# A two-layer decoder kernel: another order of the attention steps, other top-k rounds, paired value products and more warming matmuls

## The chip, the cores and the metric

The kernel runs on one core of one Trainium2 chip. The metric is the device time of a launch in microseconds (us). The core has a matrix engine (TensorE; PE in the profile, and PEld for its weight loads), a vector engine (VectorE, DVE), an activation engine (ScalarE, ACT), a general engine (GpSimd, POOL) and queues that start DMA transfers, of which SyncE's (SP) carries nearly all.

## The reference

The input is 512 tokens of 1024 channels in float32. Layer 0 is attention, layer 1 a spatial gating unit; behind each stands a gated feed-forward network (FFN) with a short causal convolution, and a final norm ends it. The change lies in layer 0's attention, which mixes two parts and projects their concatenation:

```python
h = rmsnorm(x, g)
proj = h @ w_in
aq, ak, av, ar, alr, bq, bk, bv, iq, ik, iw = split_cols(proj, IN_WIDTHS)
log_a = jax.nn.log_sigmoid(alr @ w_a2 + b_a) / GLA_GATE_TAU
oa = gla_chunked(aq, ak, av, log_a)                 # gated linear attention, 4 heads
oa = rmsnorm(oa, head_g) * jax.nn.silu(ar)
bq, bk, iq, ik = (rope_partial(a, pos) for a in (bq, bk, iq, ik))
# sparse attention, 8 heads that share one key and one value of width 64
score = sum_h iw[h] * relu(iq[h] @ ik.T)            # 4 indexer heads, causal
idx = top_k(score, 128)                             # the keys that a query may see
ob = softmax(bq @ bk[idx].T / 8) @ bv[idx]
x = x + concat([oa, ob]) @ w_o
```

## The kernel before

Activations lie with channels on the 128 partitions and the 512 tokens along the row. Weights come in chunks of 128 x 1024 on SP's queue, two chunks ahead of their use; ScalarE casts each to a high part (L148) and VectorE, or GpSimd for the names in `ON_POOL`, subtracts to get the low part (L149). A product of float32 numbers is then three matmuls (L160 to L162). Buffers: two raw chunks, three pairs of parts, four PSUM banks for long accumulations (`pacc`) and four for short ones (`paux`).

A few matmuls on zeros come first (`WARM`, L111). Four chunks of w_in give the indexer's queries and keys, the key, the value and some narrow columns (`p_first`). Each further chunk of w_in is taken by `chan` (one bank, 24 matmuls of 512 columns) or, four chunks at a time, by `tokens` (four banks at once, 96 matmuls).

The steps of the attention are named, with the token block or tile as a digit: QK (queries and keys of the linear attention), LG and DC (its logits and decays, `logits` and `decays`), AV (its values), ST (states), GL (its output), AR and GT (gates), BQ (queries of the sparse attention, with RoPE in `halves` and four copies on SP's queue in `queries`), SC (indexer scores), TC (top-k), W (softmax weights, `weigh`) and A (value products, `gather`). A round of top-k finds the eight largest scores of each query and strikes them out (`topk`, L349 and L350). It takes sixteen rounds for each of the token blocks 1, 2 and 3; each TC does four rounds for all three.

`ORDER` lists the steps in the order of preference. A scheduler at build time turns this list into one fixed stream of instructions per engine: it takes an instruction when a model of times says that it can run, and the list decides between those that can. So the list shifts priorities; it is not the order itself, and an engine executes its stream strictly in order. In `gather`, each pair of tiles of weights is transposed, copied out of PSUM (L541 or L543) and multiplied by the values (L545); the two products of a pair write the lower and the upper 64 partitions of one bank. `SWAPPED` names the tiles for which ScalarE and VectorE change places in `weigh` (L524 to L527) and in those copies. After the steps, `out_half` multiplies the first half of w_o with the linear attention's output and then the second half with the sparse attention's.

Of the kernel before, what the change touches and what calls it, by code (L numbers as in the profile page):

```python
# [26 lines left out]
LOOKAHEAD = 2  # L27
WARM = 9
ORDER = ("QK0 SC1 QK1 SC2 SC3 LG QK2 DC0 QK3 DC1 BQ0 BQ1 BQ2 TC2 BQ3 TC3 AV ST1 "
         "ST0 GL0 GL3 TC1 GL2 GL1 AR GT1 GT0 GT2 GT3 W0 TC0 W3 A0 W1 W2 A3 A1 A2")  # L30
MIX_LAG = 4
SPREAD = 3
# what GpSimd does in place of VectorE; where ScalarE and VectorE change places
ON_POOL = {
# [4 lines left out]
}  # L39
SWAPPED = {  # L40
# [3 lines left out]
}  # L44
# [3 lines left out]
def trunk(ctx: ExitStack, tc: tile.TileContext, I, out):  # L48
# [10 lines left out]
    paux = ctx.enter_context(tc.tile_pool(name="paux", bufs=4, space=PSUM))  # L59

    def slot(name, dt=F32):
        return spool.tile([P, T], dt, tag="s", name=name)
# [12 lines left out]

    # ---- inputs that stay
    pg = cst.tile([P, 40], F32, name="pg")
    nc.scalar.dma_start(pg, I["gains"])
    pv = cst.tile([P, I["pv"].shape[1]], F32, name="pv")
    nc.gpsimd.dma_start(pv, I["pv"])  # L80
    x = [xpool.tile([P, T], F32, tag="x", name=f"x{d}") for d in range(KD)]
    con = cst.tile([P, 3, P], F32, name="con")
    nc.gpsimd.dma_start(con, I["con"])
    ident, cmask, gmask = con[:, 0, :], con[:, 1, :], con[:, 2, :]
# [15 lines left out]
    def gate_b(i):  # L100
        o = 264 + 88 + i
        return pv[:, o:o + 1]

    one = cst.tile([P, 1], F32, name="one")
    V.memset(one, 1.0)
# [9 lines left out]

    # ---- weights: loaded in chunks of [128, 1024], each split into two float32r parts
    order = []
    for name, n in (("w_in", 20), ("w_o", 8), ("w_up0", 44), ("w_dn0", 24), ("w_uv", 16),
                    ("w_out", 8), ("w_up1", 44), ("w_dn1", 24)):
        for c in range(n):  # L120
            cols = 768 if name.startswith("w_dn") and c % 3 == 2 else 1024
            if name.startswith("w_dn"):
                src = I["w_dn"][int(name[4]), c // 3][:, 1024 * (c % 3):1024 * (c % 3) + cols]
            elif name.startswith("w_up"):
                src = I["w_up"][int(name[4]), c]
            else:
                src = I[name][c]
            order.append((f"{name}_{c}", src, cols))
    ready = {}
    state = {"made": 0, "used": 0}  # L130

    def make_chunk():
# [6 lines left out]
        if i < 4:  # L139
            for k2 in range(2):  # L140
                w = slice(k2 * T, (k2 + 1) * T)
                nc.sync.dma_start(x[2 * i + k2], I["xT"][2 * i + k2])
                nc.sync.dma_start(raw[:, w], src[:, w])
                S.copy(h[:, w], raw[:, w])
                V.tensor_sub(l[:, w], raw[:, w], h[:, w])
        else:
            nc.sync.dma_start(raw[:, :cols], src)
            S.copy(h[:, :cols], raw[:, :cols])  # L148
            eng(name).tensor_sub(l[:, :cols], raw[:, :cols], h[:, :cols])  # L149
# [13 lines left out]

    # ---- the normed stream: x * gain in two parts, and 1/rms of each token
    class Normed:
# [25 lines left out]
    def residual(d, ps, step):  # L191
        """x[d] += ps, then the next norm's step on it; the last one is what all wait for."""
        with tc.high_priority() if d == KD - 1 else nullcontext():
# [29 lines left out]
    def chan(n, name):  # L223
        """A chunk's 128 channels by all tokens, before 1/rms."""
        wh, wl = chunk()
# [10 lines left out]
    def tokens(n, name):  # L236
        """Four chunks' 512 channels, by blocks of tokens, before 1/rms."""
        ps = [acc(f"{name}{b}") for b in range(NB)]
# [13 lines left out]

    # ---- layer 0: attention
    n0 = normed()
# [12 lines left out]
    lo, hi = slice(0, 64), slice(64, P)  # L267
    CS = [slot("rope_c"), slot("rope_s")]
    for i in range(2):
        nc.gpsimd.dma_start(CS[i], I["rope"][i])  # L270

    def halves(ps, cs, name):
        """A tile after its rotation, in two parts."""
        t1 = slot("rope1")
# [12 lines left out]
    def queries(ps, cs, dst, name):  # L287
        """dst[e] = head e's high part over its low part."""
        h, l = halves(ps, cs, name)
# [4 lines left out]
    def dots(ps, q, ks):  # L294
        """All four products of the parts."""
        PE.matmul(ps, q, ks[0], start=True, stop=False)
# [28 lines left out]

    mask = [cmask]

    def scores(b):
        n = P * (b + 1)
        t = slice(b * P, (b + 1) * P)  # L330
        sc = slot(f"score{b}")
        mask.append(sc[:, :n])
        for h in range(4):
# [20 lines left out]

    # gated linear attention
    def queries_keys(i):
# [144 lines left out]

    # sparse attention
    def heads(i):
# [25 lines left out]
    def gather(b):  # L529
# [3 lines left out]
        for st in range(b + 1):  # L533
            pT = []
            for e in range(2):
# [4 lines left out]
                if bool(e) != (f"pT{b}{st}{e}" in SWAPPED):  # L540
                    S.copy(pT[e], pt)  # L541
                else:
                    V.tensor_copy(pT[e], pt)  # L543
            for e in range(2):
                PE.matmul(po[64 * e:64 * e + 64, :], tok[:, st, 0:64], pT[e], start=st == 0, stop=st == b)  # L545
        split(lazy("bh", [P, 4, T], F32R)[:, :, t], lazy("bl", [P, 4, T], F32R)[:, :, t],
              po.rearrange("p (j c) -> p j c", c=P))

    picked = [0] * NB
    # the steps of layer 0 in the order that the scheduler prefers  # L550
    steps = {"QK": queries_keys, "SC": scores, "LG": logits, "DC": decays, "BQ": heads, "AV": values,
             "ST": states, "GL": gla, "AR": gates, "GT": gate, "W": weigh, "A": gather,
             "TC": lambda i: topk((1, 2, 3), 4)}
    for name in ORDER.split():
        step = steps[name.rstrip("0123")]
        i = name[len(name.rstrip("0123")):]
        step(int(i)) if i else step()

# [17 lines left out]

    # ---- gated conv FFN
    def ffn(l, n, nxt, gi):
# [52 lines left out]
    def close(n, ps, t):  # L631
        """The last residual, final norm and store of 256 tokens."""
        with tc.high_priority():
# [35 lines left out]

    # ---- layer 1: spatial gating  # L670
    v = [big(f"v{b}", [P, 2, T]) for b in range(NB)]
# [66 lines left out]
def _layout(inp):  # L738
# [6 lines left out]
    def by_k(w):  # L745
        """[K, n] -> [128, K / 128, n]"""
        return w.reshape(w.shape[0] // P, P, w.shape[1]).transpose(1, 0, 2)
# [35 lines left out]
    A["w_s"] = f["sgu_w_s"][0].transpose(2, 0, 1)  # L783
    # constants of the shapes
    i = np.arange(P)
# [33 lines left out]
```

## Time and profile before

| | us |
|---|---|
| median of three runs | 1124.99 |
| lowest and highest run | 1124.42, 1126.47 |
| profiled execution, span | 1124.9 |
| TensorE busy | 1099.9 |
| VectorE busy | 717.1 |
| ScalarE busy | 451.2 |
| GpSimd busy | 100.8 |

The profiled execution is told by its span alone, from the first to the last instruction; the page has no other time of it. The first 257.5 us are layer 0's attention, the rest the two FFNs and layer 1.

How to read the rows further down: a row of a timeline has the start in the span, the busy time, the engine, the line, the operation and its tiles and how many instructions are merged (x2); in brackets stands how long the engine was idle before, and what ended that. A row of stretches has, for each engine, the busy time and the number of instructions, then TensorE's granted clock as a share of 2.4 GHz, the DMA engines' busy share and GB/s. Matmuls overlap in the records, so their pitch is read from their starts or their count.

### The profile page before, as it was taken

Reading aid. Unit: us, or ns where it says so; the run is one execution under the profiler, and the core shown is the slowest. Engines: PE = TensorE matmul, PEld = TensorE weight load, DVE = VectorE, ACT = ScalarE, POOL = GpSimd, SP = SyncE. Lnnn points to the kernel's source line nnn. Section 1 sums busy time; section 2 is a strip of 40 time slices with the busy share of each in tenths; the row PEclk is TensorE's granted clock in tenths of the full one; section 3 lists DMA queues with packets and bytes.
Section 4 is the critical chain, followed back from the end, with each engine's and each line's share of the span. In section 5 each row is a group of like instructions: output and inputs, shape, how many; then the busy total and the mean of one; then the engine's idle time right before and its main releaser. Section 6 shows DMA issues by size and latency. Waiting matters only on the chain.

```text
span 1124.9 us, 13026 instructions
## 1 busy us (share of the span) xinstructions
PE 1099.9 (98%) x5043; PEld 893.1 (79%) x5043; DVE 717.1 (64%) x1112; ACT 451.2 (40%) x649; POOL 100.8 (9%) x71
## 2 busy tenths in 40 slices
PE   8997999999999999999999999999999999999997
PEld 6875767487888888888888888888888888888886
DVE  5799789667777777753333385766777777753222
ACT  6452249144444444432222333435444444433221
POOL 1454240040000000000000000120000000000001
PEclk9998999999999999999999999999999999999999
DMA  6615120122222332223333523222233322233322
GB/s 225 187 38 150 57 68 9 38 94 94 94 94 95 103 102 95 94 85 103 99 94 108 169 75 113 76 94 94 94 96 104 100 94 94 94 103 87 101 85 75
DMA packets 34925, 108.86 MB, mean 97 GB/s; under 512 B 4160, under 2 KB 6480, under 8 KB 34864
## 3 DMA queue, kind: packets, MB, share of 16 engines
q1 hardware_dynamic: 33536, 104.87, 29.4%
q10 hardware_dynamic: 1040, 2.27, 0.7%
q8 instruction: 39, 0.64, 0.2%
q0 software_dynamic: 288, 0.90, 0.2%
q14 instruction: 22, 0.18, 0.0%
HBM read 101.73 MB, written 2.10 MB: 92 GB/s over the span
## 4 chain that ended last, share of the span: by engine, by line
PE 92%; DVE 5%; ACT 1%; issue 1%; DMA 0%; POOL 0%; POOLq 0%; SPq 0%; DVEq 0%; ACTq 0%
PE p_up L161 14%; PE p_up L162 14%; PE p_up L160 14%; PE p_dn L162 7%; PE p_dn L161 7%; PE p_dn L160 7%; PE po L545 1%; PE p_v L246 1%; PE p_so L160 1%; PE p_so L161 1%; PE p_u L160 1%; PE p_v L248 1%; PE p_u L161 1%; PE p_so L162 1%; PE p_u L162 1%; PE p_v L247 1%
## 5 line engine op out<-in xcount | busy, mean ns | idle before, releaser
L160 PE MATMUL p_up<-xh,h_w_up 128*128 128x512 f32 x704 | 274.3, 390 | 0.7 <-ACT xh L173 0.7
L161 PE MATMUL p_up<-xl,h_w_up 128*128 128x512 f32 x704 | 274.0, 389 | 0.6 <-DVE xl L174 0.6
L162 PE MATMUL p_up<-xh,l_w_up 128*128 128x512 f32 x704 | 273.9, 389 | 0.0
L160 PEld LDWEIGHTS p_up<-xh,h_w_up 128*128 128x128 f32 x704 | 132.1, 188 | 28.3 <-ACT xh L173 1.1
L161 PEld LDWEIGHTS p_up<-xl,h_w_up 128*128 128x128 f32 x704 | 132.1, 188 | 28.3 <-DVE xl L174 0.9
L162 PEld LDWEIGHTS p_up<-xh,l_w_up 128*128 128x128 f32 x704 | 132.1, 188 | 27.4
L161 PE MATMUL p_dn<-g,h_w_dn 128*128 128x512 f32 (+1 forms) x374 | 140.9, 377 | 0.0
L160 PE MATMUL p_dn<-g,h_w_dn 128*128 128x512 f32 (+1 forms) x374 | 140.9, 377 | 0.0
L162 PE MATMUL p_dn<-g,l_w_dn 128*128 128x512 f32 (+1 forms) x374 | 140.9, 377 | 0.0
L149 DVE TENSOR_TENSOR l_w_dn<-raw_w_dn,h_w_dn 128x1024 fp32r<-128x1024 f32 (+1 forms) x48 | 54.5, 1136 | 107.7 <-ACT h_w_dn L148 107.6
L148 ACT CAST h_w_up<-raw_w_up 128x1024 fp32r<-128x1024 f32 x88 | 92.7, 1054 | 62.5 <-PE p_up L161 47.7
L587 DVE TENSOR_TENSOR a<-p_up,R 128x512 f32<-128x512 f32 x88 | 60.5, 688 | 84.5 <-PE p_up L162 79.3
L149 DVE TENSOR_TENSOR l_w_up<-raw_w_up,h_w_up 128x1024 fp32r<-128x1024 f32 x87 | 106.5, 1224 | 9.4 <-ACT h_w_up L148 7.0
L148 ACT CAST h_w_dn<-raw_w_dn 128x1024 fp32r<-128x1024 f32 (+1 forms) x48 | 47.2, 983 | 147.8 <-PE p_dn L161 143.4
L160 PEld LDWEIGHTS p_dn<-g,h_w_dn 128*128 128x128 f32 x374 | 70.4, 188 | 13.0
L161 PEld LDWEIGHTS p_dn<-g,h_w_dn 128*128 128x128 f32 x374 | 70.4, 188 | 12.9
L162 PEld LDWEIGHTS p_dn<-g,l_w_dn 128*128 128x128 f32 x374 | 70.4, 188 | 12.8
L599 ACT CAST g<-c 128x512 fp32r<-128x512 f32 x44 | 27.3, 621 | 116.8 <-DVE c L596 116.8
L589 ACT ACTIVATE c<-a,pv 128x512 f32<-128x512 f32 x88 | 71.7, 815 | 2.9 <-DVE a L587 2.3
L592 DVE SCALAR_TENSOR_TENSOR c<-a,pv,c 128x510 f32<-128x510 f32 x88 | 65.9, 749 | 3.0
L590 DVE SCALAR_TENSOR_TENSOR c<-a,pv,c 128x511 f32<-128x511 f32 x88 | 65.6, 745 | 1.8 <-ACT c L589 1.8
L595 ACT ACTIVATE c<-c 128x512 f32<-128x512 f32 x44 | 27.8, 632 | 82.6 <-DVE c L592 82.6
(259 smaller groups left out, 1620.2 us busy)
## 6 DMA issues: line engine op xcount, KB each, us to landing
raw_w_up<-in_w_up SPq DMA_DIRECT2D x88, 512.0 KB, 3.3
raw_w_dn<-in_w_dn SPq DMA_DIRECT2D x32, 512.0 KB, 3.4
raw_w_in<-in_w_in SPq DMA_DIRECT2D x16, 512.0 KB, 3.6
raw_w_uv<-in_w_uv SPq DMA_DIRECT2D x16, 512.0 KB, 3.4
raw_w_dn<-in_w_dn SPq DMA_DIRECT2D x16, 384.0 KB, 3.1
raw_w_o<-in_w_o SPq DMA_DIRECT2D x8, 512.0 KB, 3.3
raw_w_out<-in_w_out SPq DMA_DIRECT2D x8, 512.0 KB, 3.4
x<-in_xT SPq DMA_DIRECT2D x8, 256.0 KB, 5.1
```

What stands on the lines that cost most here:

```text
L148: S.copy(h[:, :cols], raw[:, :cols])
L149: eng(name).tensor_sub(l[:, :cols], raw[:, :cols], h[:, :cols])
L160: PE.matmul(ps, wh, xh, start=start, stop=False)
L161: PE.matmul(ps, wh, xl, start=False, stop=False)
L162: PE.matmul(ps, wl, xh, start=False, stop=stop)
L246: PE.matmul(ps[b], n.h[k][:, t], wh[:, w], start=k == 0, stop=False)
L587: V.tensor_mul(a, ps, n.R)
L589: S.activation(cc, a, AF.Identity, bias=conv_b(l, m), scale=conv_w(l, m, 2))
L590: V.scalar_tensor_tensor(cc[:, 1:], a[:, :T - 1], conv_w(l, m, 1), cc[:, 1:], op0=ALU.mult, op1=ALU.add)
L592: V.scalar_tensor_tensor(cc[:, 2:], a[:, :T - 2], conv_w(l, m, 0), cc[:, 2:], op0=ALU.mult, op1=ALU.add)
L595: S.activation(c[0], c[0], AF.Silu)
L599: S.copy(gh, c[1])
```

## The change

It warms with 20 matmuls where there were 9. The order of steps is another one, and TC gives way to steps T that name their blocks (T12 does four rounds for blocks 1 and 2). The chunks of w_in are loaded by the order in which the new list uses them. Constants, RoPE tables and per-channel values are loaded on SP's queue behind the third chunk, no longer on GpSimd's. The first product of a pair in `gather` also waits for the second tile's copy. Two lists of who computes what have other members.

```diff
-WARM = 9
-ORDER = ("QK0 SC1 QK1 SC2 SC3 LG QK2 DC0 QK3 DC1 BQ0 BQ1 BQ2 TC2 BQ3 TC3 AV ST1 "
-         "ST0 GL0 GL3 TC1 GL2 GL1 AR GT1 GT0 GT2 GT3 W0 TC0 W3 A0 W1 W2 A3 A1 A2")
+WARM = 20
+ORDER = ("QK0 LG BQ2 SC2 SC1 T12 QK1 BQ3 QK3 QK2 DC1 DC0 SC3 BQ0 AV ST0 BQ1 ST1 GL0 GL1 "
+         "T123 GL2 T23 GL3 AR GT1 GT0 T1 T23 GT2 GT3 W0 T3 W3 T1 W1 W2 A1 A3 A2 A0")
...
 ON_POOL = {
-    "gate0", "gate2", "gate3", "ka0", "ka1", "qa1", "qa2", "rabq1", "rabq2",
-    "rabq3", "rakk", "rcs0", "rcs1", "rmiq1", "rsbq0", "rsbq2", "rsbq3", "rsiq0",
-    "ss2", "ss3", "w_in_10", "w_in_11", "w_in_12", "w_in_14", "w_in_15", "w_in_17", "w_in_18",
-    "w_in_4", "w_in_8", "w_o_0", "w_o_1", "w_o_5", "w_up0_1",
+    "gate0", "gate2", "gate3", "ka1", "qa2", "rabq1", "rabq3", "raiq1", "rcs1", "rmbq0",
+    "rmbq2", "rmbq3", "rmiq0", "rmiq1", "rmkk", "rsbq0", "rsbq1", "rsiq0", "ss3",
+    "w_in_12", "w_in_15", "w_in_18", "w_in_4", "w_in_6", "w_in_7", "w_in_9", "w_o_0",
+    "w_o_1", "w_o_3", "w_o_5", "w_o_6",
 }
 SWAPPED = {
-    "nm01", "nm02", "nm03", "nm10", "nm12", "nm13", "nm14", "nm16", "nm22",
-    "nm24", "nm25", "nm30", "nm32", "nm33", "nm34", "pT001", "pT101", "pT111",
-    "pT200", "pT201", "pT211", "pT221", "pT301", "pT311", "pT321", "pT331",
+    "nm03", "nm14", "nm33", "pT111",
 }
...
+    def together(i, other):
+
+        tc.add_manual_dep(i.ins, other.ins.name,
+                          mybir.DependencyInfo(mybir.DependencyClass.Sync, mybir.DependencyReason.DATA),
+                          reason="together")
...
+    at = {"QK1": [5], "QK2": [6], "QK3": [7], "BQ0": [8], "BQ1": [9], "BQ2": [10], "BQ3": [11],
+          "AV": [12, 13, 14, 15], "AR": [16, 17, 18, 19]}
+    order[5:20] = [order[i] for name in ORDER.split() for i in at.get(name, ())]
...
+            if i == 2:
+                for t, src in ((con, I["con"]), (CS[0], I["rope"][0]), (CS[1], I["rope"][1]), (pv, I["pv"])):
+                    nc.sync.dma_start(t, src)
...
             for e in range(2):
-                PE.matmul(po[64 * e:64 * e + 64, :], tok[:, st, 0:64], pT[e], start=st == 0, stop=st == b)
+                i = PE.matmul(po[64 * e:64 * e + 64, :], tok[:, st, 0:64], pT[e][0], start=st == 0,
+                              stop=st == b)
+                if e == 0:
+                    together(i, pT[1][1])
```

## Rows read from the trace of the kernel before

**Rows 1.** The page's totals: busy us, share of the span and instructions of each engine

```profile
PE 1099.9 (98%) x5043; PEld 893.1 (79%) x5043; DVE 717.1 (64%) x1112; ACT 451.2 (40%) x649; POOL 100.8 (9%) x71
```

**Rows 2.** Stretches, by stage: PE, PEld, DVE, ACT, POOL, PEclk, DMA share, GB/s

```profile
30.90:80.00 49.10, 49.02 (x215) 38.83 (x213) 40.44 (x60) 27.81 (x44) 23.56 (x15) 0.97 0.38 104
80.00:107.00 27.00, 18.78 (x59) 13.72 (x59) 27.00 (x65) 5.42 (x7) 15.89 (x10) 0.81 0.53 148
107.00:163.90 56.90, 56.27 (x342) 42.21 (x340) 47.20 (x140) 15.86 (x45) 16.74 (x11) 1.00 0.21 65
163.90:169.20 5.30, 2.43 (x19) 2.05 (x19) 4.60 (x8) 3.57 (x6) 3.05 (x2) 1.00 0.39 131
169.20:228.50 59.30, 59.23 (x279) 38.21 (x280) 44.70 (x150) 29.92 (x85) 2.40 (x1) 1.00 0.07 25
...
257.50:1124.90 867.40, 859.27 (x3911) 715.18 (x3909) 515.03 (x642) 336.41 (x415) 22.80 (x19) 1.00 0.31 97
```

**Rows 3.** Stretches right behind pauses of TensorE, and one of steady products

```profile
7.38:10.98 3.60, 3.60 (x10) 2.82 (x10) 2.17 (x4) 2.47 (x5) 0.00 (x0) 0.57 1.04 407
11.00:30.80 19.80, 19.80 (x88) 16.43 (x87) 14.23 (x23) 12.16 (x20) 2.40 (x1) 0.99 0.60 206
...
93.10:97.00 3.90, 3.69 (x8) 2.46 (x8) 3.90 (x11) 1.19 (x2) 1.78 (x2) 0.56 0.42 97
100.80:107.00 6.20, 6.17 (x15) 4.85 (x16) 6.20 (x20) 1.67 (x2) 3.99 (x4) 0.51 0.71 226
```

**Rows 4.** Timeline of TensorE at the start

```profile
1.23 3.71 PE L112 MATMUL ps_warm<-warm 128*128 128x512 bf16 x9 [1.23 <-DVE mhalf L114]
7.38 0.82 PE L160 MATMUL p_first<-xh,h_w_in 128*128 128x512 f32 x2 [2.44 <-ACT h_w_in L144]
```

**Rows 5.** Timeline of TensorE, 78 to 132 us: the rows with a pause ahead

```profile
80.99 0.50 PE L162 MATMUL p_bq<-xh,l_w_in 128*128 128x512 f32 x1 [0.92 <-POOL l_w_in L149]
...
93.18 0.78 PE L246 MATMUL p_av<-h_w_in,xh 128*128 128x512 f32 x1 [3.72 <-DVE rope L278]
...
98.91 0.50 PE L248 MATMUL p_av<-l_w_in,xh 128*128 128x512 f32 x1 [2.04 <-DVE l_w_in L149]
100.83 0.79 PE L246 MATMUL p_av<-h_w_in,xh 128*128 128x512 f32 x1 [1.42 <-DVE rope L278]
```

**Rows 6.** Timeline of VectorE, 64 to 82 us: logits, decays, the first query tile

```profile
64.59 3.30 DVE L393 SCALAR_TENSOR_TENSOR z<-z,ez 128x512 f32<-128x512 f32 x2
...
70.06 1.72 DVE L400 TENSOR_TENSOR bm<-bcum 128x512 f32<-128x512 f32 x1
71.70 0.68 DVE L403 TENSOR_TENSOR bl<-bcum 128x512 f32<-128x512 f32 x1
...
81.41 0.68 DVE L277 TENSOR_TENSOR rope<-p_bq,rope_rc 128x512 f32<-128x512 f32 x1
```

**Rows 7.** Groups by line, 0 to 260 us: the top-k rounds; busy us, mean ns

```profile
L350 DVE MATCH_REPLACE8 score<-m,score 128x256 f32<-128x256 f32 (+2 forms) x48 | 25.7, 540 | 0.0
L349 DVE MAX8 m<-score 128x8 f32<-128x256 f32 (+2 forms) x48 | 24.9, 546 | 0.0
```

**Rows 8.** Timeline of ScalarE: a cast behind the query copies

```profile
104.72 1.05 ACT L148 CAST h_w_in<-raw_w_in 128x1024 fp32r<-128x1024 f32 x1 [1.03 <-DMA raw_w_in<-in_w_in]
```

**Rows 9.** Timeline of TensorE, 160 to 225 us: value products alone and together

```profile
181.33 1.07 PE L545 MATMUL po<-pT,tok 128*64 128x512 f32 x2
...
197.66 1.08 PE L545 MATMUL po<-pT,tok 128*64 128x512 f32 x4
```

**Rows 10.** Groups by line, 0 to 260 us: ScalarE's part of the softmax weights

```profile
L522 ACT ACTIVATE pr<-pr,mx 128x128 f32<-128x128 f32 (+3 forms) x32 | 17.6, 550 | 0.5 <-DVE mx L520 0.3
...
L527 ACT ACTIVATE pr<-pr,sm 128x128 f32<-128x128 f32 (+3 forms) x11 | 5.7, 516 | 0.1
```

**Rows 11.** Timelines: the last split behind a gather, the second half's first product

```profile
223.70 0.68 DVE L445 TENSOR_TENSOR bl<-po,bh 128x512 fp32r<-128x512 f32 x1
...
228.36 0.39 PE L160 MATMUL p_o<-bh,h_w_o 128*128 128x512 f32 x1
```

More of the change, by code (lines that the diff above doesn't have):

```diff
@@ L79, in trunk @@
     pv = cst.tile([P, I["pv"].shape[1]], F32, name="pv")
-    nc.gpsimd.dma_start(pv, I["pv"])
     x = [xpool.tile([P, T], F32, tag="x", name=f"x{d}") for d in range(KD)]
     con = cst.tile([P, 3, P], F32, name="con")
-    nc.gpsimd.dma_start(con, I["con"])
     ident, cmask, gmask = con[:, 0, :], con[:, 1, :], con[:, 2, :]
@@ L102, in gate_b @@
         return pv[:, o:o + 1]
+    CS = [slot("rope_c"), slot("rope_s")]
     one = cst.tile([P, 1], F32, name="one")
@@ L267, in trunk @@
     lo, hi = slice(0, 64), slice(64, P)
-    CS = [slot("rope_c"), slot("rope_s")]
-    for i in range(2):
-        nc.gpsimd.dma_start(CS[i], I["rope"][i])
     def halves(ps, cs, name):
@@ L324, in trunk @@
     V.tensor_scalar(iw, tok[:, :, 64:68], 1.0 / 16.0, None, op0=ALU.mult)
-    mask = [cmask]
+    mask = {0: cmask}
     def scores(b):
@@ L331, in scores @@
         sc = slot(f"score{b}")
-        mask.append(sc[:, :n])
+        mask[b] = sc[:, :n]
         for h in range(4):
@@ L540, in gather @@
                 if bool(e) != (f"pT{b}{st}{e}" in SWAPPED):
-                    S.copy(pT[e], pt)
+                    pT[e] = (pT[e], S.copy(pT[e], pt))
                 else:
-                    V.tensor_copy(pT[e], pt)
+                    pT[e] = (pT[e], V.tensor_copy(pT[e], pt))
             for e in range(2):
-                PE.matmul(po[64 * e:64 * e + 64, :], tok[:, st, 0:64], pT[e], start=st == 0, stop=st == b)
+                i = PE.matmul(po[64 * e:64 * e + 64, :], tok[:, st, 0:64], pT[e][0], start=st == 0,
+                              stop=st == b)
+                if e == 0:
+                    together(i, pT[1][1])
         split(lazy("bh", [P, 4, T], F32R)[:, :, t], lazy("bl", [P, 4, T], F32R)[:, :, t],
@@ L551, in trunk @@
     steps = {"QK": queries_keys, "SC": scores, "LG": logits, "DC": decays, "BQ": heads, "AV": values,
-             "ST": states, "GL": gla, "AR": gates, "GT": gate, "W": weigh, "A": gather,
-             "TC": lambda i: topk((1, 2, 3), 4)}
+             "ST": states, "GL": gla, "AR": gates, "GT": gate, "W": weigh, "A": gather}
     for name in ORDER.split():
-        step = steps[name.rstrip("0123")]
-        i = name[len(name.rstrip("0123")):]
-        step(int(i)) if i else step()
+        step = name.rstrip("0123")
+        i = name[len(step):]
+        if step == "T":
+            topk([int(b) for b in i], 4)
+        elif i:
+            steps[step](int(i))
+        else:
+            steps[step]()
     def out_half(h, l, last, n):
```

## The prediction

> **What bounds the kernel now.** I read the totals of the page first: TensorE is busy 98% of the span, VectorE 64%, ScalarE 40%, GpSimd 9% [rows 1]. Nothing but TensorE's own stream can set the end, so I cut the span into stages by the timeline and asked for the busy times of each [rows 2]. Everything after 257.5 us is the two FFNs and layer 1, where TensorE works 859 of 867 us at a granted clock of 1.00; the change touches none of it. So the question is what TensorE loses ahead of 257.5. Three places show it. The start is one [rows 3, 4]. From 80 to 107 us it works 18.8 of 27.0 us at a mean clock of 0.81, while VectorE is busy all 27.0: the one stage where another engine bounds. From 163.9 to 169.2 us it works 2.43 of 5.3 us. Then I asked for the granted clock of the stretches around those holes [rows 3]: right after the pause at the start it was 0.57, after the two holes of the third stage 0.56 and 0.51; the kernel runs at about half clock behind a pause and at 1.00 (2.4 GHz) otherwise. Last come the timelines, which name what each hole waits for [rows 4 to 6].
>
> The sum is made against the profiled execution, whose span is 1124.9 us; the page gives it no other time. The median of the three runs is 1124.99, so 0.1 us is added at the end.
>
> **Longer warming.** Nine matmuls of zeros run from 1.23 to 4.94 us, 0.41 us apart, then TensorE stands 2.44 us for the first cast weights, and the first products start at 7.38 us [rows 4]. Ten of them fill 3.60 us at clock 0.57, where 88 fill 19.8 us at 0.99, 0.225 us each [rows 3]: ten at that pitch are 2.25 us, so the slow start costs 1.4 us; the 2.44 us stay, for the longer warming fills them. Twenty warming matmuls fill the hole: nine at 0.41 us, then (if the clock rises after as long as it took behind 7.38 us, 3.6 us) eleven at 0.225, which ends at 1.23 + 3.7 + 2.5 = 7.4 us, just where the products start today. Gain 1.4 us. If the clock doesn't rise, twenty at 0.41 end at 9.4 us: 2.0 us late, 1.4 won, so 0.6 lost. I take -1.4. The constants, the RoPE tables and pv leave GpSimd's queue for SP's, behind the third weight chunk; they are first read after the first products, and the same bytes leave in the first 20 us, so I cost this at nothing; its cover is that TensorE takes 5.4 us (24 x 0.225) for a chunk. If the fourth chunk slips behind them, about 1 us.
>
> **Order of steps and of top-k, GpSimd's list.** The holes from 80 to 107 us are 0.92, 3.72, 2.04 and 1.42 us: for a GpSimd split, a VectorE shuffle, a VectorE split, a shuffle [rows 5], 8.1 us together. The shuffles read the PSUM banks of the query projections BQ2 and BQ3, which the four value accumulators need: pacc has four banks and AV stands right behind BQ0 to BQ3. They are late because VectorE spent 64.6 to 81.4 us on the logits and decays, and met the first query tile only at 81.41 [rows 6]. Those decays were slow: bm took 1.72 us where its neighbour took 0.68, and the eight of them run from 70.06 to 81.41, 1.42 each. After the holes 8 and 15 matmuls run slow, the 15 in 6.20 us, 0.41 each [rows 3]: 23 x (0.41 - 0.225) = 4.3 us. So the stage loses 12.4 us.
>
> The new order puts LG before the queries, BQ2 and BQ3 before QK3 and QK2, only BQ0 right ahead of AV, and BQ1 behind it. The banks ahead of AV are then those of BQ3, QK3, QK2 and BQ0; the two QK ones are freed by one instruction. TensorE's work from BQ2 to the end of QK2 is 5 x 24 x 0.225 = 27 us, plus scores and logits of about 5: 32 us. VectorE's in that stretch: rounds T12, eight of two instructions, 1.09 us on the mean [rows 7] and an estimated 0.95 for these narrower blocks, 7.6 us; scores, ten instructions of up to 0.68, an estimated 5; two drains 1.4; seven rope instructions 4.9 (0.7 each); two splits of double width 2.4; logits, two at 0.68 to 1.65 and two scans of about 1.2, 3.8 to 5.7; eight decays 5.4 (at 0.68) to 11.4 (at 1.42). That is 30 to 38 us: from 2 us ahead to 6 behind. After QK2 VectorE owes a drain, two decays, SC3, a split or two and BQ0's two instructions, 8 to 10 us, before the fourth value bank is free; TensorE needs that bank after SC3, BQ0 and 18 matmuls, about 11 us. So it is 0 to 5 us late. I take 3, nearer to the disturbed end, which is what the trace shows, and for the slow clock behind a shorter hole 2 us. The stage then loses 5.0 instead of 12.4: -7.4. Ends: -12.4 and 0.
>
> GpSimd's busy time in the stretch 30.9 to 80 us is 23.6 us [rows 2], the same stretch in which the decays were slow. The list keeps fifteen small operations on it and drops two splits, so the disturbance goes on; I leave it in at the row's size. The Trainium skill says in "SBUF — State Buffer", section "Who interferes with whom", that a VectorE instruction with two SBUF inputs and a GpSimd one that reads SBUF exclude each other for a whole instruction, while one with a single SBUF input is not held. The trace agrees on bm (1.72 beside GpSimd, 0.68 without). By that rule only the two decay products left on GpSimd would stretch VectorE's decays, the term would be some 3 us better, -10.4, and the rounds would never be held.
>
> The chunks by order of use only keep each load with its step. But every query step puts four copies on SP's queue that wait for rope results, ahead of the next weight load; today one cast waits 1.03 us for such a load [rows 8]. At worst that is four times, 4.1 us; I take 0, since raw has two buffers and a load waits for its release longer than for a copy.
>
> **Value products side by side.** gather runs ten pairs of products into the lower and upper 64 partitions of one bank. Five pairs are issued together and take 1.08 us, like the row at 197.66; five pairs run one after the other, each half 1.07 us, like the row at 181.33 [rows 9]. (The timeline has five rows of four records and ten of two.) The new wait holds the first product until the second copy is done, so all ten run together: 5 x 1.0 = -5.0 us, all on TensorE's stream, which is 59.23 of 59.3 us busy there [rows 2]. Behind the waiting product on TensorE stand the next transposes or p_o products; at worst five pairs wait a copy of 0.6 us, so -2.0. Against that wait: nineteen of the twenty copies are on VectorE now and one on ScalarE, eleven and nine after, so the two copies of a pair mostly run at once.
>
> **ScalarE and VectorE change places.** In weigh, ScalarE normalises 11 of 32 tiles (0.52 us each), after it 17: 3.1 us more on an engine that carries 17.6 us of exponentials ahead of them [rows 10]. It is hidden by the 21.6 us (96 x 0.225) of p_o products of the first half, of which TensorE still has 4.0 us left when the last gather is split: that ends at 224.4 us, the second half starts at 228.36 [rows 11]. With 5 us less of paired products that cover is gone, and a part of the 3.1 us shows. I take +1.0; ends 0 and +3.1.
>
> **Sum.** -1.4 - 7.4 - 5.0 + 1.0 = -12.8; 1124.9 - 12.8 + 0.1 = 1112.2 us. The rest (sums of squares on VectorE, w_o splits) lies beside a full TensorE: 0, within 1 us each way.
>
> **Rivals.**
> 1. The hole before AV only moves: VectorE, whose work is the same sum in a new order, is as late for BQ0 as it was for BQ3. For it: it is 100% busy in that stage. Against: two of the four banks come free by one instruction. Then -1.4 - 5.0 + 1.0 = -5.4: 1119.6.
> 2. All stalls of this layer go: -1.4 - 12.4 - 5.0 and the 2.9 us from 163.9 to 169.2: -21.7, 1103.3. For it: VectorE is idle 9.7 of 56.9 us from 107 to 163.9. Against: the gates' chain there runs through GpSimd either way.
> 3. Slower: the rounds T1 and T23 stand between GT0 and GT2. If VectorE is behind, these (four at 0.8 and eight at 1.1 to 1.4, 13 us) hold the splits of GT2 and GT3, without which no p_o product can start, and TensorE has nothing else. Price 13 us instead of the 2.9 lost there now, plus 4.3 us slow clock, and the old hole stays: -5.4 + 10.1 + 4.3 = +9.0, 1134.0. It decides from about 6 us of rounds left behind the last AR product. For it: VectorE is busy 78.8 of the 89.2 us from 80 to 169.2 [rows 2], and the gains forecast above would leave it about 80. Against: it starts the rounds earlier, and has AR's 21.6 us with little else to do.
> 4. The pairs don't pair: other instructions stand between the halves, or the added wait costs what it gains. -7.8: 1117.2.
>
> **How the numbers follow.** Forecast 0.40, rival 1 0.20, rival 2 0.10, rival 3 0.16, rival 4 0.08, and 0.06 for gains and losses that cancel within 0.2% (2.2 us, about what a measurement of this kernel can tell from no change). Faster 0.78, same 0.06, slower 0.16. The forecast's own range is 1106 to 1119 (-1.4 to +0.6, -12.4 to -3, -5 to -2 and 0 to +3.1, not all at one end). To hold 8 in 10 it reaches to rival 1 and on to no change above, and to rival 2 below: 1102 to 1125.5; rival 3 is left out.
>
> **What would show it.** Right: no pause of TensorE from 5 to 7.4 us and clock 1.00 from the first product; ten rows of four records in gather and none of two; holes of under 4 us before the value products, and one slow stretch at most. Wrong: p_first starting after 8 us; pauses of 8 us or more anywhere from 60 to 110 us; a pause of over 5 us between the gate products and the first p_o.

## The result, and the profile after

The changed kernel takes 1118.16 us (median of 20 executions, 1110.70 to 1128.04), the kernel before 1125.42 us (20 executions, 1122.62 to 1127.56): a ratio of 0.9927, 95% interval 0.9910 to 0.9945. The ratio leaves out the two slowest executions of the changed kernel, which lie over 1.5% above its fastest. It is faster, by 7.3 us where 12.8 were forecast.

Those 20 times do not lie around one value. Each execution is recorded with its mean granted TensorE clock, and the times follow it: seven lie from 1110.7 to 1112.1 us at 0.992 to 0.994, seven from 1118.1 to 1119.9 at 0.985 to 0.987, six from 1124.4 to 1128.0 at 0.976 to 0.981. The kernel before has no such groups: its 20 times lie within 5 us, and its clock, as the experiments' runs of it recorded, was 0.990 to 0.993. The size fits: a mean clock of 0.987 or 0.980 instead of 0.994 is worth an estimated 7.8 or 15.6 us (0.007 and 0.014 of some 1116 us), and the times at these clocks lie 7.3 and 15.0 us apart (medians 1110.8, 1118.2 and 1125.8). The trace of after is from the first group (span 1108.9 us, 1.8 us around it); the experiments had to show where in the kernel the slow clock stands.

The page's totals of after (engine, busy us, share of the span, instructions):

```profile
PE 1089.9 (98%) x5054; PEld 889.8 (80%) x5054; DVE 701.6 (63%) x1105; ACT 458.2 (41%) x663; POOL 83.6 (8%) x60
```

The stretches of after, columns as in [rows 2]. The same clock times hold later work now, because everything has moved forward:

```profile
30.90:80.00 49.10, 47.60 (x214) 38.24 (x213) 38.53 (x75) 25.07 (x39) 23.56 (x17) 1.00 0.47 133
80.00:107.00 27.00, 24.62 (x132) 19.53 (x132) 25.81 (x59) 8.89 (x14) 7.60 (x4) 1.00 0.41 127
107.00:163.90 56.90, 52.71 (x301) 38.10 (x300) 46.22 (x143) 21.02 (x60) 17.84 (x12) 0.94 0.18 61
```

From 80 to 107 us TensorE is busy 24.62 us at clock 1.00, against 18.78 at 0.81 [rows 2]. The next stretch loses more than it did: TensorE is busy 52.71 of its 56.9 us at 0.94, against 56.27 at 1.00. TensorE's timeline of after says why (start, length, then the row; in brackets the pause ahead and what ended it):

```profile
1.22 5.94 PE L115 MATMUL ps_warm<-warm 128*128 128x512 bf16 x20 [1.22 <-DVE mhalf L117]
6.81 0.58 PE L170 MATMUL p_first<-xh,h_w_in 128*128 128x512 f32 x1
...
86.77 0.50 PE L256 MATMUL p_av<-h_w_in,xh 128*128 128x512 f32 x1 [2.02 <-DVE rope L285]
115.07 0.49 PE L474 MATMUL ps_o<-av,at 128*128 128x128 f32 x2 [1.52 <-DVE at L463]
154.95 2.18 PE L505 MATMUL pt_oa<-con,oa 128*128 128x128 f32 x16 [1.33 <-DVE oa L502]
158.16 0.33 PE L303 MATMUL ps_qk<-key,bq 128*128 128x128 f32 x1 [1.03 <-DVE al L452]
...
190.88 1.08 PE L552 MATMUL po<-pT,tok 128*64 128x512 f32 x4
194.26 1.94 PE L552 MATMUL po<-pT,tok 128*64 128x512 f32 x8
...
211.96 1.08 PE L552 MATMUL po<-pT,tok 128*64 128x512 f32 x4 [0.57 <-ACT pT L548]
213.73 1.21 PE L170 MATMUL p_o<-bh,h_w_o 128*128 128x512 f32 x4 [0.69 <-ACT bh L451]
```

The start has no pause, one pause of 2.02 us is left before the value products in place of four [rows 5], and all ten pairs are rows of four or eight records. New is the pause at 115.07, in the gated linear attention, for VectorE's masked product `at`. And behind it the clock falls; stretches of the same trace:

```profile
113.50:116.60 3.10, 1.58 (x9) 0.97 (x8) 3.10 (x13) 0.62 (x1) 2.10 (x2) 1.00 0.54 178
116.60:123.30 6.70, 6.70 (x20) 4.43 (x19) 2.91 (x9) 1.25 (x8) 1.03 (x1) 0.52 0.28 64
123.30:153.60 30.30, 30.30 (x173) 22.08 (x172) 23.48 (x70) 10.33 (x32) 9.85 (x7) 0.99 0.13 46
```

For 6.7 us TensorE is busy without a gap at 0.52, about 1.2 GHz: 6.7 x 0.48 = 3.2 us lost. VectorE's timeline shows the decays and the queue ahead of `at`:

```profile
74.28 0.68 DVE L407 TENSOR_TENSOR bm<-bcum 128x512 f32<-128x512 f32 x1
...
75.48 1.29 DVE L419 TENSOR_TENSOR qa<-qa,qk 128x512 f32<-128x512 f32 x2
76.70 1.76 DVE L419 TENSOR_TENSOR ka<-ka,qk 128x512 f32<-128x512 f32 x1
...
112.29 0.69 DVE L286 TENSOR_TENSOR rope<-rope,rope_rs 128x512 f32<-128x512 f32 x1
112.89 0.69 DVE L356 MAX8 m<-score 128x8 f32<-128x512 f32 x1
...
113.75 0.68 DVE L357 MATCH_REPLACE8 score<-m,score 128x512 f32<-128x512 f32 x1
...
114.60 0.42 DVE L463 TENSOR_TENSOR at<-ps_at,con 128x256 f32<-128x256 f32 x1
```

The product that `at` reads was issued by 112.2 us; rounds of T23 and BQ1's rotation, moved behind the value products, stand between.

### The profile page after: what moved, and what is told of

Read it like the earlier page. It is cut to its first block, busy times and chain, and to the rows that moved or that the text cites. A ratio compares the mean times of both kernels' runs of the same rounds, so it can differ in the third digit from the quotient of the medians.

```text
span 1108.9 us, 13034 instructions
## 1 busy us (share of the span) xinstructions
PE 1089.9 (98%) x5054; PEld 889.8 (80%) x5054; DVE 701.6 (63%) x1105; ACT 458.2 (41%) x663; POOL 83.6 (8%) x60
## 4 chain that ended last, share of the span: by engine, by line
PE 55%; issue 33%; DVE 8%; DMA 1%; POOL 1%; ACT 0%; SPq 0%; POOLq 0%; DVEq 0%; ACTq 0%
PE p_up L172 7%; PE p_up L171 7%; PE p_up L170 7%; PE p_dn L171 4%; PE p_dn L172 4%; PE p_dn L170 4%; DVE score L357 2%; DVE m L356 1%; PE p_o L171 1%; PE p_v L256 1%; PE p_so L170 1%; PE p_so L171 1%; PE p_u L170 1%; PE p_u L172 1%; PE p_v L258 1%
## 5 line engine op out<-in xcount | busy, mean ns | idle before, releaser
L170 PEld LDWEIGHTS p_dn<-g,h_w_dn 128*128 128x128 f32 x374 | 70.4, 188 | 12.8
```

Source lines behind the costliest of these rows:

```text
L170: PE.matmul(ps, wh, xh, start=start, stop=False)
```

## The experiments

Each was timed beside the kernel before on the same chip; a ratio is to that kernel. "At the same clock" compares executions with the same mean granted clock.

**e1: the kernel before, twenty warming products.**

```diff
-WARM = 9
+WARM = 20
```

> The kernel before with twenty warming products instead of nine, nothing else. My account of the change: the 2.44 us pause at the start is filled and the first products run at 0.225 us instead of 0.41, so the end comes 1.4 us earlier by the sum, up to 2.1 us by the trace of after (its first bank's end moved from 30.86 to 28.80 us); ratio 0.9981 to 0.9988. Rival A, that the earlier start is given back in the first later stage that waits for VectorE (80 to 107 us): 0, ratio 1.000. Rival B, that the longer warming is what gives the changed kernel its several times some 7 us apart: this kernel's own runs spread over 7 us or more as well, where the runs of before stay within 5.

Measured: 1126.56 us, ratio 1.0001 (0.9992 to 1.0010). Rival A holds; B does not, for all 11 executions lie from 1124.4 to 1127.5. TensorE's timeline of e1:

```profile
1.23 7.42 PE L112 MATMUL ps_warm<-warm 128*128 128x512 bf16 x20 [1.23 <-DVE mhalf L114]
8.29 0.58 PE L160 MATMUL p_first<-xh,h_w_in 128*128 128x512 f32 x1
...
92.91 0.80 PE L246 MATMUL p_av<-h_w_in,xh 128*128 128x512 f32 x1 [3.73 <-DVE rope L278]
98.63 0.49 PE L248 MATMUL p_av<-l_w_in,xh 128*128 128x512 f32 x1 [2.23 <-DVE l_w_in L149]
```

The warming ran at the slow pace nearly throughout (20 in 7.42 us), so the first product came later than before (8.29 against 7.38 [rows 4]) but at full pace; the first sum-of-squares product starts 0.6 us earlier (30.26, before 30.86). The holes for VectorE's shuffle and split end 0.3 us earlier than they did [rows 5] and take half of it back; the first p_up product comes 0.5 us earlier (249.65, before 250.12), which the times don't show.

**e2: the kernel before, the added wait alone.** The diff is `together` and its one call, on the old order, lists and places.

> The kernel before with the added wait alone (the first value product of a pair waits for both copies), ScalarE and VectorE in their old places. Account of the prediction: all ten pairs run side by side, five of them 1.0 us shorter, so -5.0 us (ratio 0.9955); in the trace ten rows of four records in the gather stage and none of two. Rival (the pairs don't pair, or the wait costs what it gains, because nineteen of twenty copies are on VectorE): 0 to -2.0 us, with pauses of TensorE of 0.6 us ahead of the pairs. Rival (the gain is hidden behind ScalarE's weights and exponentials): pairs side by side, and the pause before the second half's first product grows by as much, 0 us.

Measured: 1119.86 us, ratio 0.9942 (0.9931 to 0.9954), so -6.5 us. The first products of the softmax weights start at 168.2 us as before, the first p_up at 244.0 instead of 250.1 us: -6.1 in the trace. TensorE's timeline of e2, where all ten pairs stand in such rows (two of them in one row of eight records):

```profile
182.45 1.08 PE L550 MATMUL po<-pT,tok 128*64 128x512 f32 x4
```

It is more than the forecast 5.0: a half alone takes as long as a pair (1.07 and 1.08 [rows 9]), and each of the five interruptions that go also saves some 0.1 us at either end (a p_o product before a value product starts 0.32 us ahead of it instead of 0.23).

**e3: the changed kernel, nine warming products.** `WARM = 9`.

> The changed kernel with nine warming products instead of twenty. My account: the start falls back to 7.38 us with about ten products at half clock, +1.4 to +2.1 us (ratio to before about 0.9945 in place of 0.9927 over all runs), and its runs still lie some 7 us apart from each other, because what sets them apart is the clock behind the 1.5 us pause at 115 us. Rival B: the spread comes from the longer warming, so all runs lie within 5 us of each other, near 1113.

Measured: 1119.89 us (1112.27 to 1128.28, 12 executions), ratio 0.9954 (0.9928 to 0.9981). The groups stay, so rival B falls. At the same clock it equals the changed kernel: 1112.3 at 0.992, 1119.1 to 1120.0 at 0.985. Its trace is from a slower execution (span 1115.9 us, clock 0.989) and shows where the time goes. TensorE's timeline, then stretches:

```profile
116.25 0.49 PE L474 MATMUL ps_o<-av,at 128*128 128x128 f32 x2 [1.56 <-DVE at L463]
```

```profile
114.70:118.40 3.70, 2.15 (x11) 1.51 (x11) 3.70 (x14) 1.10 (x5) 2.08 (x2) 0.98 0.48 156
118.40:138.40 20.00, 20.00 (x71) 13.12 (x69) 8.01 (x26) 3.06 (x15) 2.04 (x2) 0.50 0.09 20
138.40:160.40 22.00, 22.00 (x122) 16.63 (x118) 17.65 (x54) 7.86 (x22) 8.62 (x6) 0.99 0.18 58
```

The same pause (1.56 us) is followed by 20 us at 0.50 instead of 6.7 at 0.52: 10.0 us lost instead of 3.2. The difference, 6.8 us, is about the distance of the two spans (7.0) and of the first two groups (1111.7 and 1118.2 by their medians). But 0.989 lies between these groups; e8's trace (below) is at the clock of the second, and no trace is from the third.

**e4: the changed kernel without the wait.** The two lines `if e == 0: together(...)` are gone.

> The changed kernel without the added wait; the pairs' copies stay where the change put them (one of a pair on each engine). If the wait is what pairs the products: rows of two records come back in the gather stage, up to ten pairs at 2.1 in place of 1.1 us; +5 us if five of them split, +1 us for each pair. If the exchanged copies pair them by themselves: 0 to +1 us, still mostly rows of four records. Rival C, that the wait costs pauses on TensorE in the gather stage: -0.5 to -1.5 us.

Measured: 1117.03 us (1115.43 to 1132.58), ratio 0.9947 (0.9919 to 0.9974); at a clock of 0.992 and more 1116.5 (seven executions) against 1111.7: the wait is worth 4.8 us here too. TensorE's timeline of e4:

```profile
189.53 1.07 PE L552 MATMUL po<-pT,tok 128*64 128x512 f32 x2
...
206.30 1.38 PE L552 MATMUL po<-pT,tok 128*64 128x512 f32 x4
```

Only two pairs split altogether, but the eight others overlap only in part, at 1.14 to 1.87 us instead of 1.08, since the second copy comes late. Rows of four records are not yet pairs in step: the duration says it.

**e5 and e12: eight products ahead of the waiting one.**

```diff
             ps = aux(f"ps_o{b}{e}")
+            if b == 0 and e == 0:
+                for _ in range(8):
+                    PE.matmul(ps, keys[0][0][:, :P], keys[0][0], start=True, stop=True)
```

> The changed kernel with eight products that nobody reads (128 x 512, operands that are long ready) ahead of the first product of the gated attention that waits 1.5 us for VectorE at 115 us. Theory (the pause is what lowers the clock, for 7 us in one execution and 20 us in another, and so sets the several times of the changed kernel): no idle slice at 115 us, granted clock 1.00 from 107 to 164, and all runs within 3 us of each other near 1108 to 1109 (the best of the changed kernel, 1111, less 3.3 us of slow clock, plus 0.3 for eight products that take longer than the pause); ratio 0.985. Rival (the many small products of this stage lower the clock by themselves, pause or none): the slow stretch of 7 to 20 us stays, times spread from 1111 to 1128 as before, +0.3 us. Rival 2 (other steps lower it): all times shifted alike, spread the same, slow stretch elsewhere.

> The kernel of e5 once more, for a trace (e5's three undisturbed times were 1114 to 1116 at a mean clock of 0.990). Theory of the pause: no idle slice at 115 us and clock 1.00 behind it, so what is lost against 1109 stands as a new pause and a slow stretch at another place of this layer. Rival: the slow stretch at 117 us is there although the pause is filled.

Measured: e5 1114.3 to 1116.3 us in three executions (ratio 0.9911, 0.9896 to 0.9925) and 4658.5 us in a fourth, whose trace is the one kept and is not read; e12 1112.9 and 1113.1 (0.9894, 0.9873 to 0.9916). TensorE's timeline of e12, and a stretch of it:

```profile
117.09 2.11 PE L473 MATMUL ps_o<-key 128*128 128x512 f32 x8 [1.38 <-DVE at L464]
```

```profile
123.30:153.60 30.30, 30.30 (x176) 23.00 (x176) 25.07 (x70) 10.16 (x31) 9.97 (x7) 1.00 0.13 39
```

The test missed its aim: the eight write to a bank that comes free with `at`, so they ran behind the pause, not in it. What it shows instead is that a pause of 1.38 us followed by large products left the clock at 1.00 from 116.6 to 153.6 us in that execution, and that these five executions lie from 1112.9 to 1116.3 us, where only seven of twenty of the changed kernel are so fast. The 2.1 us of the eight, a pause for `oa` grown from 1.33 to 3.39 us, and 3.4 us lost to slow clock at two other places (from 88 and from 156 us) kept it from 1109.

**e6: T23's first rounds behind `at`.**

```diff
-                V.max(m8, mask[b])
+                i = V.max(m8, mask[b])
+                if r == 0 and behind:
+                    tc.add_manual_dep(i.ins, behind.ins.name, ... NoSync, SCHED_ONLY ...)
...
-            topk([int(b) for b in i], 4)
+            topk([int(b) for b in i], 4, gated.get(0) if 2 in gated and 3 not in gated else None)
```

> The changed kernel with the first rounds of T23 ordered on VectorE behind the first block's masked product (at) of the gated attention; no work added. Between the value drains and that instruction 5.3 us of rounds leave VectorE's queue, 2.0 us of them after its operand is ready at 112.2 us. Theory: the pause of 1.5 us at 115 us shrinks to under 0.5 us, no slow clock behind it, runs within 3 us near 1107 (1111 - 3.3 - 1.5), if the rounds find room in the 10 us that VectorE idles from 107 to 164. Rival (other work of VectorE, BQ1's rotation and the state updates, holds it as long): pause 1 us or more and the same spread, 1111 to 1128. Rival 2 (the rounds moved back hold the gates' splits): no pause at 115, but over 5 us between the gates and the first output product, 1112 or more in all runs.

Measured: 1114.53 us, ratio 0.9919 (0.9893 to 0.9945); five of six executions from 1113.6 to 1115.3 at 0.996, one at 1124.1. A stretch of e6, then TensorE's, VectorE's and GpSimd's timelines:

```profile
110.00:140.00 30.00, 28.66 (x196) 19.61 (x195) 22.52 (x62) 7.43 (x36) 7.95 (x7) 1.00 0.19 53
```

```profile
113.66 0.49 PE L481 MATMUL ps_o<-av,at 128*128 128x128 f32 x2 [0.93 <-DVE at L470]
...
170.54 0.50 PE L303 MATMUL ps_qk<-key,bq 128*128 128x512 f32 x1 [1.92 <-DVE mx L534]
```

```profile
167.13 2.41 DVE L365 TENSOR_SCALAR score<-score 128x512 f32<-128x512 f32 x1
```

```profile
166.88 2.38 POOL L159 TENSOR_TENSOR l_w_o<-raw_w_o,h_w_o 128x1024 fp32r<-128x1024 f32 x1 [13.59 <-DVE score L362]
```

With the pause cut from 1.52 to 0.93 us the slow clock of this stage is gone, and with it most of the spread. Not the time: by the gates e6 is 3.1 us ahead of the changed kernel (pt_oa at 151.9 against 155.0), at the first p_up 2.9 us behind (238.5 against 235.7). The rounds pushed back met a GpSimd split in the attention weights: the widest mask took 2.41 us, in the changed kernel 0.40, and TensorE waited 1.92 us. Behind that wait 1.7 us went to slow clock, and pauses of 0.95, 0.83 and 0.80 us stand ahead of pairs.

**e9: half of it.** As e6 with `if r == 1 and behind`.

> As e6, but only the second and later rounds of that T23 are ordered behind the masked product: 2.6 us of rounds leave VectorE's queue ahead of it instead of 5.3. Theory: the pause at 115 us is under 1 us and no slow clock follows up to 164 us, runs within 3 us of each other; and as half as many rounds are late, the waits for the attention weights that e6 showed (mx 1.9 us at 170 us, three of 0.8 to 1.0 us ahead of the pairs) are half or gone: 1106 to 1111, faster than the changed kernel's best 1111. Rival (any shift of the rounds comes back in the weights): 1113 to 1115 as e6. Rival 2 (too few leave: the pause stays over 1 us): slow clock and the spread again.

Measured: 1114.00 us, ratio 0.9933 (0.9886 to 0.9979): four of six at 1113.5 to 1114.1, two at 1122.0 and 1128.4. The clock is 1.00 behind the pause at 116 us (0.93 long). But the 2.02 us pause before the value products, harmless in the trace of after, was followed by slow clock here, a stretch of e9:

```profile
88.20:92.90 4.70, 4.70 (x14) 3.71 (x15) 3.52 (x10) 1.88 (x4) 3.09 (x3) 0.64 0.09 22
```

and pauses of 1.95 us for `al` and 1.54, 0.83 and 0.81 us ahead of pairs took the rest. The rival holds: rounds put off come back in the weights.

**e10: e6 with one w_o split on VectorE.** `"w_o_1"` leaves `ON_POOL`.

> As e6, with one split of w_o (chunk 1) on VectorE instead of GpSimd. In e6 the mask of the widest block (one SBUF operand, 128 x 512) took 2.41 us beside a GpSimd split of 2.38 us, where it takes 0.40 in the changed kernel, and TensorE then waited 1.92 us with some 1.5 us lost at half clock behind. Theory (the two shut each other out, that is e6's loss): no split of GpSimd runs beside the mask, it takes 0.40 us, TensorE's wait of 1.92 us is gone, 1110 to 1111. Rival (VectorE is simply short of time for the rounds moved back): the wait stays at 1.5 us or more, for 1.2 us of split come on top, 1113 to 1116.

Measured: 1116.49 us (four within 0.9), ratio 0.9926 (0.9909 to 0.9944). In its trace the mask stands beside no split and takes 0.42 us, and TensorE's 1.92 us wait is gone, as the theory said; the time is not, for waits of 1.00 us (a residual sum) and 1.18 us (a copy) and a slow stretch from 159 to 167 us stand in its place. In these runs, what was taken from one hole opened another.

Taken together, e6, e9 and e10 have the pause for `at` at 0.93 us, with the clock at 1.00 behind it in all three traces, and 13 of their 16 executions lie from 1113.5 to 1117.1 us. What made the other three slower (1122 to 1128 us, clock 0.978 to 0.987) no trace shows.

**e7: the kernel before with the new order alone.** New `ORDER` and T steps, chunks in order of use, constants on SP's queue; `WARM`, `ON_POOL`, `SWAPPED` as before, no wait.

> The kernel before with the new order of steps and rounds, the chunks in order of use and the constants on SP's queue; nine warming products, no added wait, GpSimd's list and the places of ScalarE and VectorE as before. The prediction's sum gives this part -7.4 us (ratio 0.9934), my reading of the two traces -7.6 us in the executions with the shortest slow stretch (12.4 lost before the value products gone, 1.5 and 3.3 lost anew in the gated attention) and 0 in those with the longest, so several times again, some 7 us apart, from 1116 to 1130. Rival (without the new GpSimd list the new order does not close the hole): a pause of 3 us or more before the value products and a time of 1122 or more in every run.

Measured: ratio 1.0107 (1.0081 to 1.0134), 12 us slower: 1134.3 to 1134.9 us in three executions, 1142 in two. The rival's time holds, by more than it said. Its pause can't be read here, for the trace is of an execution of 1570 us, at a clock of 0.655 throughout; e11 shows the place.

**e11: the changed kernel with GpSimd's old list.**

> The changed kernel with GpSimd's list of before (twenty-seven names, of which twenty-three still exist), all else as changed. From e7 (the new order with old lists 9 us slower than before, where the sum had -7.4): theory, the order pays only with the new list, so this is 8 to 12 us slower than the changed kernel at the same clock (1120 to 1123 in its best executions), with a pause of TensorE of 3 us or more ahead of the value products or the weights, for a GpSimd result. Rival (what cost e7 its time is the pairs and the places, not the list): within 3 us of the changed kernel.

Measured: 1130.96 us (1123.68 to 1136.44), ratio 1.0044 (1.0020 to 1.0068): 12.8 us slower than the changed kernel by the medians, 13.0 by the best executions. (The list put back has thirty-three names, not twenty-seven, and all of them exist in the changed kernel.) TensorE's, VectorE's and GpSimd's timelines of e11:

```profile
86.54 0.66 PE L258 MATMUL p_av<-l_w_in,xh 128*128 128x512 f32 x1 [2.97 <-DVE l_w_in L159]
92.59 0.80 PE L256 MATMUL p_av<-h_w_in,xh 128*128 128x512 f32 x1 [4.96 <-DVE rope L285]
```

```profile
80.21 1.77 DVE L419 TENSOR_TENSOR ka<-ka,qk 128x512 f32<-128x512 f32 x1
81.90 1.78 DVE L410 TENSOR_TENSOR bl<-bcum 128x512 f32<-128x512 f32 x1
83.60 1.75 DVE L419 TENSOR_TENSOR qa<-qa,qk 128x512 f32<-128x512 f32 x1
...
86.41 2.84 DVE L419 TENSOR_TENSOR ka<-ka,qk 128x512 f32<-128x512 f32 x1
```

```profile
79.21 2.22 POOL L419 TENSOR_TENSOR qa<-qa,qk 128x512 f32<-128x512 f32 x1 [4.48 <-ACT qa L412]
81.39 3.41 POOL L419 TENSOR_TENSOR ka<-ka,qk 128x512 f32<-128x512 f32 x2
85.35 3.35 POOL L159 TENSOR_TENSOR l_w_in<-raw_w_in,h_w_in 128x1024 fp32r<-128x1024 f32 x1 [0.55 <-ACT h_w_in L158]
```

The old list puts three of the decays' products and a split on GpSimd beside VectorE's decays; those take 1.75 to 2.84 us each instead of 0.68, and VectorE's split and shuffle for the value products are late by as much: pauses of 2.97 and 4.96 us, against one of 2.02.

**e8: the changed kernel with the old places of ScalarE and VectorE.** `SWAPPED` is the old set of 26.

> The changed kernel with the 26 places of before where ScalarE and VectorE change. Prediction's term: the new places cost +1.0 us (0 to +3.1), so this is 0 to 3.1 us faster than the changed kernel in executions with the same clock: the pause of 0.7 us ahead of the second half's first output product goes. Rival (with nineteen copies on VectorE the added wait now costs time, since both copies of a pair go one behind the other): pauses of about 0.6 us ahead of up to five pairs, +1 to +3 us. The spread of the runs stays, for it comes from the pause at 115 us.

Measured: 1121.18 us, ratio 0.9969 (0.9956 to 0.9981). At a clock of 0.985, four executions at 1121.1 to 1121.3 against 1119.85 (one of the changed kernel; e3's four lie from 1119.1 to 1120.0): the new places win some 1.3 us. The two traces agree: from the gates' transposes to the first p_up e8 takes 81.7 us, after 80.7. The rival holds; TensorE's timeline of e8:

```profile
221.95 1.08 PE L554 MATMUL po<-pT,tok 128*64 128x512 f32 x4 [0.79 <-DVE pT L552]
223.72 1.19 PE L172 MATMUL p_o<-bh,h_w_o 128*128 128x512 f32 x4 [0.69 <-ACT bh L453]
```

With both copies of a pair on VectorE the wait costs 1.1 us in two pauses (0.34 at 202.53, and the one shown), where the changed kernel has one of 0.57; and the 0.69 us ahead of the second half stands here as well. e2, with the same copies and the same wait in the old order, has no such pause, so the copies and the wait alone don't make it.

This trace is of an execution at 0.985, the clock of the second group. Its stretch with the gated attention:

```profile
107.00:163.90 56.90, 54.20 (x265) 38.54 (x263) 39.08 (x114) 15.06 (x44) 16.55 (x11) 0.79 0.18 55
```

The clock there is 0.79, in the trace of after 0.94: behind a pause of 1.38 us for `at`, TensorE runs some 24 us at 0.51.

## Why the prediction was right, and where not

The median, 1118.16 us, lies in the range and on the forecast side; 6.0 us above the forecast, which the best executions (1111.7) meet to 0.5 us. That they meet it is in part luck: nearly every term of the sum was off, some one way and some the other, as told below. Rival 1's 1119.6 is nearer to the median, but not by its mechanism: the hole before the value products did not move to another shuffle, it shrank.

**Longer warming, -1.4.** In the trace of after the first sum of squares starts 2.06 us earlier (28.80 against 30.86), so the sign looked right. The cause was wrong: with nine products (e3) it starts at 28.6, because the first weights are cast earlier (first product at 6.63 us, before at 7.38), and at the same clock e3 is as fast. Alone in the kernel before (e1) the longer warming gives nothing. Nor is the 2.06 us a fixed gain: in the other traces with the new start and twenty products the warming takes 5.8 to 7.5 us, the first product starts as it ends (6.66 to 8.31 us), and the sum of squares starts at 28.66 to 30.31. Why the first weights are cast 0.7 to 1.2 us earlier in e1, in after and in the experiments on it (5.5 to 6.1 us; before and e2 6.7), in e1 with the constants still on GpSimd's queue, stays open.

**Order, top-k, GpSimd's list, -7.4.** The step that failed is a piece of this term: "for the slow clock behind a shorter hole 2 us", priced before the value products only, with "one slow stretch at most" as the sign. The hole there went further than forecast: idle time and slow clock fell from 12.0 to 2.0 us between the first value product and the end of those products, and 1.7 us of slow clock at 59 us went with it. But the work moved out of the way, BQ1's rotation and rounds, stands ahead of `at`, and I had costed nothing in the gated attention. From the end of the value products to the gates' transposes TensorE loses 6.6 us in the trace of after (3.2 idle, 3.4 by the clock) where it lost 1.9, and 6.9 (e3) or 8.1 us (e8) beyond that when the clock stays low. In the trace of after the part comes to -8.2 up to the gates (pt_oa at 154.95 against 165.20, less the 2.06 of the start). Behind them it costs: from pt_oa to the first p_up after takes 80.7 us where the kernel before with the wait alone (e2) takes 78.8, and pauses for `al`, `mx`, `pT` and `bh` are 1.0 us of that. Over all executions the slow clock took back about what separates 1111.7 from 1118.2.

**GpSimd's list within that term.** I left the disturbance of the decays "in at the row's size" and put the other reading, "some 3 us better, -10.4", into sentences beside the sum. That reading was the right one: at the hole itself 10.0 us went. The Trainium skill ("SBUF — State Buffer", section "Who interferes with whom") has VectorE instructions with two SBUF inputs and GpSimd instructions that read SBUF exclude each other. The traces agree: 0.68 us with GpSimd idle, 1.75 to 2.84 beside its products and split (e11), in the trace of after only the one ka at 1.76. Without the new list the new order loses time (e7, 1.0107; e11, 1.0044), so one sum for both hid that the order needs the list; the new list in the old order was not run.

**Pairing, -5.0.** Right, and under-sized: -6.5 alone (e2), 4.8 in the changed kernel (e4), where one copy on each engine already brings the halves close. Rival 4 falls.

**Places, +1.0.** Wrong in sign: -1.0 by the traces, about -1.3 by the times (e8). The cover that I saw go did go (0.69 us ahead of the second half), but with the old places too; what I missed is that the added wait can make a second copy on VectorE visible.

**Rivals 2 and 3.** Not all stalls went (154.95 and 158.16 us are the gates' and splits' waits of before, 2.4 us), and T1 and T23 between the gates held no split for long. The first p_up comes 14.5 us earlier, the end 16.0: two waits of TensorE there, 0.7 and 0.6 us for the normed stream, are gone; they are back in e11 (0.9 and 0.6), so the list is their cause, which I had put at nothing.

No run here is shown to be faster than the changed kernel: e12 has the best ratio (0.9894), but its interval meets that of the change, and it has two executions.

## What to carry to other kernels

An order of work and the list that says which engine does it must be priced together: the changed kernel was 13 us slower with the old list (e11), which made a gain of 7 us into a loss. Price a new pause with the clock behind it, which cost more (3 to 12 us) than the pause itself (1.5 us), and look at many executions with their granted clocks before one trace is believed. A wait that only makes two products start together is cheap where their copies run on two engines.

## What the runs showed of the hardware

Behind the same pause for `at`, 1.4 to 1.6 us, the granted clock was low (0.50 to 0.52, the 1.2 GHz level) for 6.7 us in one execution (after), 20 us in another (e3) and some 24 us in a third (e8), with TensorE busy in every slice; it worked on small products (64 rows, or 128 columns) with full ones of 512 columns between them. Behind 1.38 us and eight full products it stayed at 1.00 (e12), and behind 0.93 us as well (e6, e9, e10). The 2.02 us pause before the value products had no slow clock behind it in the traces of after, e3, e4 and e6, and cost 1.7 us by slow clock in e8, e9, e10 and e12 (e9: 4.7 us at 0.64). And the clock fell without a pause, so the prediction's reading, about half clock behind a pause and 1.00 otherwise, was too narrow: in the kernel before, TensorE was busy throughout, with two products of only 16 rows from 55.68 and two from 57.40 us, and then ran at half clock:

```profile
55.60:59.20 3.60, 3.60 (x10) 1.55 (x10) 3.60 (x10) 2.99 (x6) 0.91 (x2) 0.99 0.03 9
59.20:62.50 3.30, 3.30 (x9) 2.53 (x9) 1.85 (x4) 3.27 (x6) 0.00 (x0) 0.50 0.00 0
```

e2 shows the same, but in e1 the same four products were followed by a clock of 1.00. Whether small products lower the clock, or keep it low, was not isolated.

A VectorE instruction with one SBUF operand (the mask, e6) was held as long as the GpSimd split beside it, 2.41 and 2.38 us. The narrower mask of 384 columns took 2.50 us in e11 and 2.07 in e12 beside a split, and 0.34 in e10 with GpSimd idle. The Trainium skill ("SBUF — State Buffer", section "Who interferes with whom") says that such an instruction can contend for the shared ports when it runs in a mode that uses two, an exception that the prediction's sentence on a single SBUF input leaves out. The rows agree on the hold; the mode they don't name. The rounds were not held beside such a split: a MATCH_REPLACE8 of 512 took 0.67 us in the trace of after from 149.82, while GpSimd's split ran from 149.13 to 151.54.
